# A five-buffer ring for the mixer outputs and x, and a split moved to GpSimd, in an S5/pooling diffusion step

## The chip, the core and the metric

The kernel runs on one core of one Trainium2 chip. The metric is device time in microseconds. A core has five engines that run their own instruction streams and meet through semaphores: TensorE (PE in the profile, with PEld for its weight loads), VectorE (DVE), ScalarE (ACT), GpSimd (POOL) and SyncE (SP), which here only issues DMAs. DMAs can be issued by SP, ACT and POOL. The matmul and vector instructions of one engine run in the order in which they stand in its stream, and that order is fixed when the kernel is built.

## The reference

Two token groups run through two layers: 128 context tokens and 1024 latent tokens, 1024 channels each, fp32.

```
for i in 0, 1:
    h = x * (1 + scale) + shift                       # adaLN, from silu(c) @ ada_w
    if i == 0:  s5 scan both ways, y = gelu(C s + D u)
                v = y @ glu_w + glu_b                 # 1024 -> 2048
                o = v[:, :1024] * sigmoid(v[:, 1024:])
    else:       multi-scale box means of h, minus h, times small weights
    x = layer_norm(4**0.25 * x + gate1 * o)
    f = (silu(m(x) @ w_gate) * (m(x) @ w_up)) @ w_down   # 1024 -> 2816 -> 1024
    x = layer_norm(4**0.25 * x + gate2 * f)
```

Outputs are both groups' x and the context's final scan states.

## The kernel before

The latent tokens are handled in two halves of 512, blocks A and B. The large products of A and B run on TensorE in a split form: each fp32 operand is written as a high part in fp32r (ScalarE, L828) plus a low part (VectorE, L829), and `mm` (L842 to L848) issues three matmuls, high x high (L844), high x low (L845), low x high (L846). The context block C (128 tokens) uses plain fp32 (L848); an fp32 matmul or transpose appears in the profile as two PE instructions.

The scan of layer 0 ends in `ssm_y`, called for the eight channel blocks in the order 6, 7, 5, 0, 1, 2, 3, 4. Each call forms y for all 1024 tokens, and eight DMAs on GpSimd's queue (L686) store it in the DRAM tensor yd[kt]. All of its tiles are in one memory pool (ssy), closed after the last call.

Then `build` opens the pools of the next stages in the memory that the scan leaves: split weights (wh, wl, three buffers), X (the residual stream), lat (work tiles of A and B, among them the ring hk of split hidden activations, three buffers of a high and a low part), xm (A's split operand) and glup. In glup lie xn (B's split operand) and the ring yr of two buffers of 128x1024 fp32. The loop at L1197 loads yd[k] for k = 0 to 7 in turn by GpSimd's queue (L1199) and splits it: tokens 0 to 511 into xm, tokens 512 to 1023 into xn, each with one ScalarE copy and one VectorE subtraction, 128x512, written with a stride of 8 elements since the scan's token order differs.

The gated unit (`glu`, L892) then takes A and B through eight output blocks m. A block m loads two weight tiles of 512 KB into the ring `raw` (three buffers, SP's queue, L837), splits them, and runs 2 x 8 x 3 = 48 matmuls of 512 columns over k = 0 to 7. Its result is gated (tile sg, two buffers) and added to X. For A, `load_x` (L410) is called at m = 0 for token tiles 0 to 3 and at m = 3 for tiles 4 to 7: each loads 128 rows of x into a buffer of the same ring `raw`, by SP's queue (L416), and TensorE transposes it (px, L421) into X.

Beside the gated unit runs `fill`: the context's feed-forward of layer 0, a generator stepped at points in the program (18 steps stand ahead of A's gated unit). In the gated unit it loads its weights, in pieces of 256 KB, into its own ring rc of three buffers (L1293). A tile framework orders the instructions when the kernel is built: by program order as priority, among those that its own timeline says are ready. It also adds the waits, among them that the tiles of a new pool wait for the pools whose memory they take.

After the gated unit come layer norm, up projection and down projection of A and of B (`ffn_down` splits the hidden activations into hk, L948), then layer 1.

Of the kernel before, what the change touches and what calls it, by code (L numbers as in the profile page):

```python
# [11 lines left out]
F32 = mybir.dt.float32  # L12
# [3 lines left out]
OP = mybir.AluOpType  # L16
# [25 lines left out]
class Kernel:  # L42
# [367 lines left out]
    def load_x(self, qs):  # L410

        nc = self.nc
        xs = self.I["x_sample"].rearrange("o n d -> (o n) d")
        for q in qs:
            xp = self.raw.tile([128, 1024], F32, tag="raw", name=f"xr{q}")
            nc.sync.dma_start(xp, xs[128 * q:128 * q + 128, :])  # L416
            for kh in range(2):
                px = self.psum("px")
                for k4 in range(4):
                    kt = 4 * kh + k4  # L420
                    nc.tensor.transpose(px[:, 128 * k4:128 * k4 + 128], xp[:, 128 * kt:128 * kt + 128], self.ident)  # L421
                nc.scalar.activation(self.X[q // 4][:, 4 * kh:4 * kh + 4, 128 * (q % 4):128 * (q % 4) + 128],
                                     px.rearrange("p (k n) -> p k n", k=4), AF.Copy)
# [497 lines left out]
    def ffn_down(self, b, l, h):  # L921
        nc, I = self.nc, self.I
        wd = I["ffn_w_down"][l].rearrange("(f p) d -> p f d", p=128)
        gate = self.gate[l, 1]

        def residual(ps, m):
            nc.vector.scalar_tensor_tensor(b.x[:, m, :], ps, gate[:, b.i, m:m + 1], b.x[:, m, :],
                                           op0=OP.mult, op1=OP.add)

        if not b.split:  # L930
            for m in range(8):
                ps = self.psum("dn", b.ps)[:, 0:b.n]
                for fo, fn in ((0, 8), (8, 8), (16, 6)):
                    w = self.weight(b, wd[:, fo:fo + fn, m * 128:m * 128 + 128], [128, fn, 128])
                    for f in range(fn):
                        self.mm(b, ps, [w[0][:, f, :]], [h[:, fo + f, :]], fo + f == 0, fo + f == NF - 1)
                residual(ps, m)
                yield m
            return
        for half in range(2):  # L940
            ps = [self.psum(f"dn{m}", b.ps)[:, 0:b.n] for m in range(4)]
            for f2 in range(NF // 2):
                w = self.weight(b, wd[:, 2 * f2:2 * f2 + 2, half * 512:half * 512 + 512], [128, 2, 512])
                nq = 512 // b.n
                for q in range(2):
                    f = 2 * f2 + q
                    if q % nq == 0:
                        hh = self.split(b.tmp, h[:, f:f + nq, :], [128, nq, b.n], "hk", 3)  # L948
                    for m in range(4):
                        self.mm(b, ps[m], [t[:, q, m * 128:m * 128 + 128] for t in w],  # L950
                                [t[:, q % nq, :] for t in hh], f == 0, f == NF - 1)
                yield f2
            for m in range(4):
                residual(ps[m], half * 4 + m)
# [204 lines left out]
    def build(self):  # L1159
        tc, nc = self.tc, self.nc  # L1160
        with ExitStack() as st:
# [25 lines left out]
            xr = P("xres")  # L1187
# [5 lines left out]
            with tc.tile_pool(name="xm1", bufs=1) as xmp:  # L1193
                xm = [xmp.tile([128, 8, 512], F32R, name=f"xm{q}") for q in range(2)]
                with tc.tile_pool(name="glup", bufs=1) as tmp:
                    xm2 = [tmp.tile([128, 8, 512], F32R, name=f"xn{q}") for q in range(2)]
                    for k in range(8):  # L1197
                        yr = tmp.tile([128, 1024], F32, tag="yr", name="yr", bufs=2)
                        nc.gpsimd.dma_start(yr, self.yd[k])  # L1199
                        yv = yr.rearrange("p (t c) -> p t c", t=8)  # L1200
                        tok = lambda a: a[:, k].rearrange("p (c t) -> p t c", t=8)
                        for q, x in enumerate((xm, xm2)):
                            self.split_into(tok(x[0]), tok(x[1]), yv[:, ::-1, 64 * q:64 * q + 64])
                    with tc.tile_pool(name="rawc", bufs=1) as self.rawc:
                        self.glu(A, xm, fill, hooks={0: range(4), 3: range(4, 8)})
                        self.glu(B, xm2, fill)
                        self.drain(fill)
                    self.rawc = None
                    self.ln(A, 0, 0, xm)
                    first = list(self.up_w(A, 0, 0))  # L1210
                self.cright.close()
                hpool = tc.tile_pool(name="ffna", bufs=1, side="right")
                h = hpool.__enter__().tile([128, NF, 512], F32, name="h")
                with tc.tile_pool(name="adl", bufs=1, side="right") as adl:
                    fill = self.ada_late(adl)
                    self.drain(self.ffn_up(A, 0, xm, h, first), fill)
                    self.ln_stats(B)
                    self.ln_apply(B, 0, 0, xm)
                    self.drain(self.ffn_down(A, 0, h), fill)
                    self.drain(fill)  # L1220
                self.drain(self.ffn_up(B, 0, xm, h))
                self.ln(A, 0, 1)
            mid, side = ExitStack(), ExitStack()
# [21 lines left out]
            xm = [xmp.tile([128, 8, 512], F32R, name=f"xp{q}") for q in range(2)]  # L1245
# [11 lines left out]
            h = st.enter_context(hp).tile([128, NF, 512], F32, name="h2")  # L1257
# [69 lines left out]
```

## Time and profile before

| | us |
|---|---|
| median of 3 runs (2425.71 to 2427.06) | 2426.21 |
| profiled execution | 2425.86 |
| its span | 2424.1 |
| PE busy | 2243.9 (93%) |
| VectorE busy | 1282.3 (53%) |
| ScalarE busy | 922.9 (38%) |
| GpSimd busy | 269.1 (11%) |

A busy share says what an engine spent its time on, not what bounded a stage. Here PE is the busy engine, and from about 541 us to the end it has little idle time; its gaps lie in the first quarter of the span, where the scan, its hand-over to the gated unit and the context's work are. Idle time of an engine other than the bound costs nothing by itself. The granted clock is TensorE's, as a share of 2.4 GHz.

### The profile page before, as it was taken

How to read it: one execution, taken by the hardware profiler on the slowest of the kernel's cores; microseconds unless marked ns; L12 is line 12 of the kernel's file. 1: busy time of each engine (PE TensorE's matmuls, PEld its weight loads, DVE VectorE, ACT ScalarE, POOL GpSimd, SP SyncE). 2: the span in 40 equal slices, each digit the busy share in tenths (PEclk: the TensorE clock that was granted, in tenths of full speed). 3: DMA queues.
4: the chain of work that ended last, by engine and by line, in shares of the span. 5: the costliest groups of instructions: out<-in, count | busy, mean ns of one | idle time of the engine just before them, and what ended most of it. 6: DMA issues, size and time to landing. Idle time of an engine off the chain costs nothing.

```text
span 2424.1 us, 33331 instructions
## 1 busy us (share of the span) xinstructions
PE 2243.9 (93%) x13105; PEld 1872.7 (77%) x13105; DVE 1282.3 (53%) x2420; ACT 922.9 (38%) x1376; POOL 269.1 (11%) x337
## 2 busy tenths in 40 slices
PE   4896679699999999999999998889999999999996
PEld 2565678688877777788888888777788888888996
DVE  6679964343555222557222765677422456322576
ACT  3674225442243222534222543226222443322464
POOL 4931336300010000100000010002000100000000
PEclk7996889899999999999999999999999999999998
DMA  7778459755544555432333226764333323333463
GB/s 223 238 238 229 140 166 262 223 177 165 150 137 149 164 183 165 167 99 87 103 98 96 96 96 174 220 196 133 105 96 96 96 97 95 96 98 102 140 200 104
DMA packets 457916, 357.22 MB, mean 147 GB/s; under 512 B 14864, under 2 KB 405792, under 8 KB 455712
## 3 DMA queue, kind: packets, MB, share of 16 engines
q1 hardware_dynamic: 451824, 340.90, 46.7%
q0 software_dynamic: 3200, 8.39, 1.1%
q10 hardware_dynamic: 2736, 5.80, 0.6%
q8 instruction: 103, 1.69, 0.3%
q14 instruction: 53, 0.43, 0.1%
HBM read 336.58 MB, written 18.35 MB: 146 GB/s over the span
## 4 chain that ended last, share of the span: by engine, by line
PE 81%; DMA 11%; DVE 3%; ACT 2%; issue 1%; POOL 1%; SPq 0%; ACTq 0%; POOLq 0%; DVEq 0%
PE ffn L844 13%; PE ffn L846 13%; PE ffn L845 13%; PE dn L845 6%; PE dn L844 6%; PE dn L846 6%; PE ffn L848 4%; PE dn L848 3%; PE glu L844 2%; PE glu L846 2%; PE glu L845 2%; DMA adaw<-ada_w 2%; DMA raw<-ffn_w_up 2%; DMA raw<-ffn_w_gate 1%; PE pvv L465 1%
## 5 line engine op out<-in xcount | busy, mean ns | idle before, releaser
L828 ACT ACTIVATE wh<-raw 128x1024 fp32r<-128x1024 f32 (+1 forms) x326 | 341.6, 1049 | 930.4 <-PE ffn L845 611.4
L829 DVE TENSOR_TENSOR wl<-raw,wh 128x1024 fp32r<-128x1024 f32 (+1 forms) x326 | 394.7, 1211 | 492.6 <-ACT wh L828 485.3
L845 PE MATMUL dn<-hkl,wh 128*128 128x512 f32 (+1 forms) x880 | 304.5, 348 | 0.3 <-DVE hkl L829 0.3
L846 PE MATMUL dn<-hkh,wl 128*128 128x512 f32 (+1 forms) x880 | 303.0, 347 | 0.0
L844 PE MATMUL ffn<-xp,wh 128*128 128x512 f32 x704 | 274.8, 391 | 2.2 <-ACT wh L828 2.2
L846 PE MATMUL ffn<-xp,wl 128*128 128x512 f32 x704 | 275.3, 391 | 0.5 <-DVE wl L829 0.5
L844 PE MATMUL ffn<-xm,wh 128*128 128x512 f32 x704 | 275.2, 392 | 0.0
L846 PE MATMUL ffn<-xm,wl 128*128 128x512 f32 x704 | 275.0, 391 | 0.0
L845 PE MATMUL ffn<-xp,wh 128*128 128x512 f32 x704 | 274.6, 391 | 0.0
L845 PE MATMUL ffn<-xm,wh 128*128 128x512 f32 x704 | 273.9, 389 | 0.0
L844 PE MATMUL dn<-hkh,wh 128*128 128x512 f32 (+1 forms) x880 | 262.5, 348 | 0.9 <-ACT hkh L828 0.9
L848 PE MATMUL ffn<-xmc,raw 128*128 128x128 f32 x1280 | 166.3, 287 | 33.7 <-DMA raw<-ffn_w_up 9.9
L918 DVE TENSOR_TENSOR h<-ffn,sg 128x512 f32<-128x512 f32 x88 | 60.7, 690 | 248.2 <-PE ffn L846 248.1
L848 PEld LDWEIGHTS ffn<-xmc,raw 128*128 128x128 f32 x1280 | 157.2, 200 | 43.9 <-DMA raw<-ffn_w_up 13.7
L845 PEld LDWEIGHTS dn<-hkl,wh 128*128 128x128 f32 x880 | 166.6, 189 | 21.1 <-DVE hkl L829 0.5
L846 PEld LDWEIGHTS dn<-hkh,wl 128*128 128x128 f32 x880 | 166.5, 189 | 20.4
L844 PEld LDWEIGHTS dn<-hkh,wh 128*128 128x128 f32 x880 | 163.3, 189 | 23.4 <-ACT hkh L828 1.7
L844 PEld LDWEIGHTS ffn<-xm,wh 128*128 128x128 f32 x704 | 132.1, 188 | 31.8 <-issue 4.3
L844 PEld LDWEIGHTS ffn<-xp,wh 128*128 128x128 f32 x704 | 132.5, 188 | 30.7 <-ACT wh L828 2.5
L846 PEld LDWEIGHTS ffn<-xp,wl 128*128 128x128 f32 x704 | 132.5, 188 | 28.9 <-DVE wl L829 1.0
L846 PEld LDWEIGHTS ffn<-xm,wl 128*128 128x128 f32 x704 | 132.1, 188 | 28.9 <-issue 0.7
L845 PEld LDWEIGHTS ffn<-xp,wh 128*128 128x128 f32 x704 | 132.4, 188 | 28.1 <-issue 0.5
(333 smaller groups left out, 3282.0 us busy)
## 6 DMA issues: line engine op xcount, KB each, us to landing
raw<-ffn_w_gate SPq DMA_DIRECT2D x128, 512.0 KB
raw<-ffn_w_up SPq DMA_DIRECT2D x128, 512.0 KB
raw<-ffn_w_down SPq DMA_DIRECT2D x126, 512.0 KB
adaw<-ada_w SPq DMA_DIRECT2D x96, 512.0 KB
raw<-ssm_glu_w SPq DMA_DIRECT2D x48, 512.0 KB
mo<-mo SPq DMA_DIRECT2D x14, 1024.0 KB
rc<-ffn_w_down SPq DMA_DIRECT2D x40, 256.0 KB
mo<-otab SPq DMA_DIRECT2D x32, 256.0 KB
```

The lines of the kernel that those rows point to most:

```text
L465: nc.tensor.matmul(pv[64 * x:64 * x + 64, 144 * r:144 * r + 144], tt[:, q, r, 64 * x:64 * x + 64], self.u[:, 2 * gp + x, :], start=True, s ...
L828: nc.scalar.activation(h, src, AF.Copy)
L829: nc.vector.tensor_tensor(l, src, h.bitcast(F32), op=OP.subtract)
L844: nc.tensor.matmul(ps, wh, xh, start=start, stop=False)
L845: nc.tensor.matmul(ps, wh, xl, start=False, stop=False)
L846: nc.tensor.matmul(ps, wl, xh, start=False, stop=stop)
L848: nc.tensor.matmul(ps, w[0], x[0], start=start, stop=stop)
L918: v.tensor_tensor(h[:, f, :], self.in_sb(b, v, pu), sg, op=OP.mult)
```

## The change

The ring yr has five buffers, stands first in its pool glup, and is reached through `self.yr`; two of its tiles are made before xn. `load_x` takes its tiles from this ring and issues its loads on GpSimd's queue. The second token half of each yd tile is split by GpSimd, with a copy and a subtraction; the first half stays on ScalarE and VectorE. The ring hk moves out of the pool lat into one of its own, on the other side of the memory, opened after the context's pools are closed and kept to the end; lat is 12 KB a partition smaller, so xm and the start of glup lie 12 KB lower, and glup, with three more buffers of 4 KB, ends where it ended.

```diff
     def load_x(self, qs):
         for q in qs:
-            xp = self.raw.tile([128, 1024], F32, tag="raw", name=f"xr{q}")
-            nc.sync.dma_start(xp, xs[128 * q:128 * q + 128, :])
+            xp = self.yr(f"xr{q}")
+            nc.gpsimd.dma_start(xp, xs[128 * q:128 * q + 128, :])
...
-                        hh = self.split(b.tmp, h[:, f:f + nq, :], [128, nq, b.n], "hk", 3)
+                        hh = self.split(self.hk, h[:, f:f + nq, :], [128, nq, b.n], "hk", 3)
...
                 with tc.tile_pool(name="glup", bufs=1) as tmp:
+                    self.yr = lambda n: tmp.tile([128, 1024], F32, tag="yr", name=n, bufs=5)
+                    yrs = [self.yr(f"yr{k}") for k in range(2)]
                     xm2 = [tmp.tile([128, 8, 512], F32R, name=f"xn{q}") for q in range(2)]
                     for k in range(8):
-                        yr = tmp.tile([128, 1024], F32, tag="yr", name="yr", bufs=2)
+                        yr = yrs[k] if k < 2 else self.yr(f"yr{k}")
                         nc.gpsimd.dma_start(yr, self.yd[k])
-                        yv = yr.rearrange("p (t c) -> p t c", t=8)
+                        yv = yr.rearrange("p (t c) -> p t c", t=8)[:, ::-1]
                         tok = lambda a: a[:, k].rearrange("p (c t) -> p t c", t=8)
-                        for q, x in enumerate((xm, xm2)):
-                            self.split_into(tok(x[0]), tok(x[1]), yv[:, ::-1, 64 * q:64 * q + 64])
+                        self.split_into(tok(xm[0]), tok(xm[1]), yv[:, :, 0:64])
+                        nc.gpsimd.tensor_copy(tok(xm2[0]), yv[:, :, 64:128])
+                        nc.gpsimd.tensor_tensor(tok(xm2[1]), yv[:, :, 64:128], tok(xm2[0]).bitcast(F32),
+                                                op=OP.subtract)
...
                 self.cright.close()
+                self.hk = st.enter_context(tc.tile_pool(name="hkp", bufs=1, side="right"))
```

## Rows read from the trace of the kernel before

**Rows 1.** Stretches of the span: each engine's busy us (instructions), granted clock, DMA share, GB/s.
```profile
core 0: us, PE busy (x) PEld busy (x) DVE busy (x) ACT busy (x) POOL busy (x), PEclk, DMA share, GB/s
...
448.80:461.68 12.88, 0.00 (x1) 0.03 (x1) 2.36 (x2) 2.02 (x3) 5.30 (x10) 0.70 0.55 167
461.68:472.00 10.32, 9.51 (x40) 8.71 (x41) 4.20 (x4) 5.21 (x6) 1.06 (x2) 0.54 0.75 235
472.00:504.00 32.00, 29.26 (x179) 24.98 (x178) 16.54 (x17) 21.60 (x26) 2.12 (x4) 1.00 0.76 238
504.00:531.00 27.00, 27.00 (x121) 22.33 (x121) 9.26 (x11) 8.61 (x10) 0.00 (x0) 1.00 0.41 124
531.00:541.20 10.20, 7.63 (x67) 7.14 (x65) 3.71 (x5) 6.49 (x11) 0.00 (x0) 1.00 0.77 228
```

**Rows 2.** PE's groups by form, 461.6 to 504: busy us, mean ns, idle before and releaser.
```profile
L848 PE MATMUL ffn<-xmc,rc 128*128 128x128 f32 x112 | 17.7, 308 | 13.7 <-DMA rc<-ffn_w_gate 12.9 <-DMA rc<-ffn_w_up 0.8
L845 PE MATMUL glu<-xm,wh 128*128 128x512 f32 x24 | 10.1, 422 | 0.4 <-DVE xm L829 0.3
L844 PE MATMUL glu<-xm,wh 128*128 128x512 f32 x25 | 9.7, 447 | 2.3 <-ACT xm L828 2.2
L846 PE MATMUL glu<-xm,wl 128*128 128x512 f32 x24 | 9.5, 394 | 0.0
L421 PE MATMUL px<-ident,xr 128*128 128x128 f32 x32 | 5.6, 317 | 0.0
```

**Rows 3.** Timeline of PE, 531 to 541: start us, us, instructions, idle before.
```profile
531.16 1.91 PE L421 MATMUL px<-ident,xr 128*128 128x128 f32 x16
...
537.67 1.06 PE L421 MATMUL px<-ident,xr 128*128 128x128 f32 x8 [1.05 <-ACT sg L916]
540.26 1.16 PE L848 MATMUL dn<-hc,rc 128*128 128x128 f32 x8 [1.52 <-DMA rc<-ffn_w_down]
541.17 0.48 PE L844 MATMUL glu<-xm,wh 128*128 128x512 f32 x1
```

**Rows 4.** The tile yr: durations in ns, minimum/median/maximum, and DMA us to landing.
```profile
L829 DVE TENSOR_TENSOR xm<-yr,xm x8: 1116/1174/1229, 466.6 to 498.9; 128x512 fp32r<-128x512 f32 x8
...
DMA to landing us min/median/max: 3.5/5.7/7.3
```

**Rows 5.** Timeline of ACT: the first and the last split of xm.
```profile
465.43 1.13 ACT L828 ACTIVATE xm<-yr 128x512 fp32r<-128x512 f32 x1 [14.61 <-DMA yr<-yd]
...
497.78 1.13 ACT L828 ACTIVATE xm<-yr 128x512 fp32r<-128x512 f32 x1 [4.28 <-DMA yr<-yd]
```

**Rows 6.** Timeline of POOL: stores of yd[0], of yd[4], and the first loads.
```profile
408.32 4.53 POOL L686 DMA_DIRECT2D yd<-yl  x8
...
451.12 4.18 POOL L686 DMA_DIRECT2D yd<-yl  x8 [3.12 <-ACT yl L683]
459.87 1.12 POOL L1199 DMA_DIRECT2D yr<-yd  x2 [4.57 <-issue]
```

**Rows 7.** Timeline of POOL, 34 to 49: two-input operations.
```profile
37.86 1.11 POOL L80 TENSOR_TENSOR oc<-pw,nct 128x512 f32<-128x512 f32 x1
...
43.37 1.96 POOL L76 TENSOR_TENSOR oc<-pw,ct 128x512 f32<-128x512 f32 x1
```

**Rows 8.** Timeline of DVE, 34 to 49: two-input operations.
```profile
38.90 1.23 DVE L77 TENSOR_TENSOR pb<-pq,bt 128x1024 f32<-128x1024 f32 x1 [1.05 <-ACT bt L318]
...
42.20 2.17 DVE L80 TENSOR_TENSOR pb<-pq,bt 128x1024 f32<-128x1024 f32 x1
```

**Rows 9.** Lines L1012 and L631: ns minimum/median/maximum, first and last start, forms.
```profile
L1012 POOL TENSOR_SCALAR lx<-X,lnm x32: 766/966/3784, 703.1 to 1911.5; 128x512 f32<-128x512 f32 x32
...
L631 POOL COPY sd<-Z x16: 1057/1562/1657, 349.1 to 441.8; 64x512 f32<-64x512 f32 x16
```

**Rows 10.** Timeline of SP's DMA queue: x tiles 4 to 7, the next glu weight.
```profile
507.82 24.73 SPq L416 DMA_DIRECT2D xr<-x_sample  x4
533.10 0.38 SPq L837 DMA_DIRECT2D raw<-ssm_glu_w  x1
```

**Rows 11.** Waits of SP's queue, 430 to 520: us in total, times, longest.
```profile
SPq L1293 <- DMA yd<-yl: 6.0, 4, 5.5
```

## The prediction, made before the change was run

> **What bounds the kernel now.** I read the table of stages first. TensorE (PE) is the bound: from 504 to 531 us it is busy all the time, 121 instructions in 27.00 us, all but one of them 512-column matmuls of the gated unit, so one costs 0.225 us at the full clock [rows 1]. The only place inside the change's reach where PE loses time is 448.8 to 541.2 us. Second view, PE's instructions by form from 461.6 to 504: 112 context-ffn and 32 transposes (fp32, 128x128) and 73 gated-unit matmuls [rows 2]. Eight fp32 ones take 540.26 to 541.17, so 0.113 each [rows 3]. Full-clock need: 144 x 0.113 + 73 x 0.225 = 16.3 + 16.4 = 32.7 us; elapsed from 461.68 to 504: 42.3. Lost: 9.6. In the first 10.32 us of it the granted clock was 0.54 [rows 1], about the 1.2 GHz level, after PE had stood for 12.88 us; at the full clock that work takes at most 10.32 x 0.54 = 5.6, so 4.7 of the 9.6 is the low clock and its gaps, and 4.9 falls between 472 and 504. From 531.2 to 541.2, PE has 64 fp32 instructions (67 less three glu): 7.2 us of work in 10.0, 2.8 lost, with two waits of 1.05 and 1.52 us, and not one glu matmul starts between 531.2 and 541.17 [rows 1, 3].
>
> So the ledger is 12.9 (PE empty) + 4.7 + 4.9 + 2.8 = 25.3 us, of a profiled execution of 2425.86 us (span 2424.1). The median of the runs is 2426.21, 0.35 above it.
>
> **The change part by part.**
>
> *Five buffers in place of two.* Eight mixer outputs yr0 to yr7 come through two buffers; each load waits until the splits of the one two before are done, then takes 3.5 to 7.3 us to land [rows 4]. So the first split starts at 465.43 and the last only at 497.78 [rows 5]: 32.4 us for eight. Five loads at once bring yr2 to yr4 forward. But the first stays where it is: yr0 reads yd[0], whose stores were issued at 408.32, and yet is issued at 459.87, right after the stores of yd[4] (issued 451.12 to 455.30) have landed [rows 6]. It waits for the memory of the stage before, not for its data; the new pool reaches into the same memory. I therefore leave the 12.9 us as they are, and with them the low clock behind them (4.7), which could shift by 1 or 2 us either way.
>
> yr0 to yr4 are issued from 459.87 on. Five times 512 KB at the 235 GB/s of that stretch [rows 1] would be 11 us, so yr4 lands by about 471. ScalarE's share falls from two splits a tile to one: 465.43 and then tile by tile to 472.
>
> *Second half split by GpSimd.* This removes eight 1.2 us instructions from ScalarE and eight from VectorE and puts sixteen on GpSimd. Neither engine is the bound, so the relief itself is worth nothing; what counts is when yr buffers come free. No row shows a GpSimd write with this 32-byte stride. From below: 1.10 us for a two-input 128x512 operation [rows 7] and 0.77 for a one-input one [rows 9], 1.9 us a tile. From above: 1.96 us each beside a busy VectorE [rows 7, 8] is 3.9, and one-input 3.78 at worst [rows 9] makes 5.9. VectorE pays for the same strided split 1.17 [rows 4], and a GpSimd copy with strided reads 1.56 [rows 9]. I take 1.5 + 1.9 = 3.4 us a tile, nearest to the strided copy.
>
> yr5 needs the first buffer, so the first tile's GpSimd split. In program order the splits of tiles 1 to 4 also stand ahead of load 5, and GpSimd works in order: if it keeps that order, yr5 to yr7 are issued at 465 + 5 x 3.4 = 482, land by 488 and are split by 490; if not, by 482. Today: 500. So the operand is whole 10 to 18 us sooner. Until then PE has tiles 0 to 4 for the first two output blocks (5 x 6 x 0.225 = 6.8 us for one, half of that again for the gate of the next) and some 80 of the fp32 context instructions (9 us) to fill about 20 us. I expect 1.5 to 3.5 us of the 4.9 to remain lost and take 2.3 as regained; from 0 to 4.9 is possible.
>
> VectorE and GpSimd also slow each other. At 38.90 a 128x1024 VectorE operation on two operands in memory took 1.23 us, at 42.20 the same form 2.17, with GpSimd at 1.96 beside it instead of 1.11 [rows 7, 8]. That is why I don't take 4.9: the low half of the A split on VectorE is in the same burst. The Trainium skill (SBUF — State Buffer, SBUF: two separate sides) says that a VectorE instruction with two SBUF inputs and a GpSimd instruction reading SBUF lock each other out for a whole instruction. The rows agree. Taken strictly, it makes a tile cost 1.17 + 3.4 = 4.6 us, load 5 goes out near 488, and nothing of the 4.9 comes back: the second rival.
>
> *x through the ring, on GpSimd's queue.* Today xr4 to xr7 take the three weight buffers in turn: SP's queue is held by them from 507.82 to 532.55, and the next glu weight is issued at 533.10 [rows 10]. That is the hole without a glu matmul [rows 3]. With weights alone in these buffers it closes: 2.8 us, between 0 (another fill order makes a like hole) and 2.8. I take 2.8. SP loses eight issues; GpSimd gains eight of the 0.56 us that its loads take [rows 6], 4.5 us behind its splits. What waits for them is the residual update of the first output block, and the two sg buffers let PE go on for two more blocks (11 us each), so x may come as late as 510 without cost. The transposes go: they no longer fill PE at 469 to 480, where the glu tiles now must. In bandwidth nothing is won: the bytes are the same. The Trainium skill (DMA: Bandwidth & Descriptors, Issuing engines are not separate DMA queues) says as much: transfers from all issuing engines share 16 DMA engines. The table shows these 0.75 busy [rows 1], so yr2 to yr4 push back the context weights; that is within my 1 or 2 us.
>
> *hk in its own pool.* The same instructions, tags and counts; nothing. Its memory is that of the context blocks, which finish beside the gated unit, a whole up projection before A's down projection needs hk. If that cover went, its first splits would wait a few us while PE is still in the up projection.
>
> Sum: 2.3 + 2.8 + 0 = 5.1. 2425.86 - 5.1 = 2420.8; against the median 2421.1. I give 2421.
>
> **Rivals.**
>
> *Memory sooner.* The ring now lies at the low end of its pool. Should its first two buffers not have to wait for the last stores, yr0 could go out at 455.3 behind them, or at 448.0 in GpSimd's gap: 4.6 to 11.9 us sooner, and PE starts on glu that much before 467. For: yd[0] is long written. Against: the context weights (rc), which have nothing to do with yd, also waited for its stores, once for 5.5 us [rows 11]. Time: 2409 to 2416.5.
>
> *Only the hole at 531.* GpSimd's splits and VectorE's take turns, yr5 to yr7 come as late as now, and the missing transposes leave PE with less to fill: 0 to 2.8 us are won. For: the slowed rows; against: three tiles more are there at 472. Time 2423 to 2426.
>
> *Slower.* GpSimd's splits cost over 5.3 us a tile. The last A split then ends at 465 + 5 x price + 8.5, which passes today's 500 from there on; at 7.6 (two of the longest, 3.78) it is 511.5, and the x loads behind it come past 515, when PE, in order, stands at their transposes and at the third output block. Loss 11.5, less 2.8, and about 2 that filler covers: 2432. For: 3.78 has happened [rows 9]. Against: the median there is 0.97.
>
> **How the numbers follow.** What a measurement of this kernel tells from no change is about 0.2%, 4.85 us: faster means below 2421.4. Forecast 0.50 (its own range 2418 to 2423.5: 0.31 faster, 0.19 same); memory sooner 0.13, faster; only the hole 0.20, same; slower 0.17 (0.16 slower, 0.01 same). Faster 0.44, same 0.40, slower 0.16. Leaving out 0.1 on either side: 2414 to 2429.5.
>
> **What would show it.** Right: yr0 to yr4 issued back to back after 459.5, the context weights still first on PE near 461.7, the last ScalarE split of A between 482 and 492, no x load on SP and no glu-free stretch of 10 us near 531. Wrong: yr0 issued before 456 (memory sooner); GpSimd splits above 5 us a tile, or PE waiting for transposes (slower); VectorE's A splits near 2.3 us with the last one after 497 (only the hole).

## The result, and the profile after

| | us |
|---|---|
| before, median beside it | 2425.96 |
| after, median of 4 runs (2438.0 to 2440.71) | 2439.32 |
| ratio after to before, 95% interval | 1.0053, 1.0040 to 1.0066 |
| measured again, 5 runs beside 11 of before | 1.0066, 1.0054 to 1.0078 |
| profiled execution after; its span | 2438.46; 2436.7 |

The change costs 13 to 16 us. The forecast was 5 us faster. Ratios here rest on undisturbed runs (an execution of 9204 us in *xr3_free* below is left out) and aren't quotients of the medians beside them, from which they can differ by a few us.

Where it goes is read from the same stretches as [rows 1]; the windows of the profile after, columns as there (its scan ends 2.2 us later, see below):

```profile
448.80:461.68 12.88, 2.22 (x20) 2.03 (x19) 3.50 (x3) 4.03 (x5) 5.65 (x11) 0.79 0.67 191
461.68:472.00 10.32, 3.75 (x16) 3.49 (x16) 0.46 (x1) 1.61 (x2) 4.33 (x7) 0.60 0.80 271
472.00:504.00 32.00, 27.10 (x156) 23.47 (x157) 11.34 (x10) 8.41 (x10) 26.71 (x20) 0.89 0.73 235
504.00:531.00 27.00, 19.32 (x114) 16.81 (x114) 5.75 (x7) 9.39 (x14) 4.18 (x6) 0.87 0.71 217
531.00:541.20 10.20, 10.20 (x46) 8.45 (x46) 3.87 (x4) 2.70 (x3) 0.00 (x0) 1.00 0.21 61
```

The hole of 531 to 541 is closed, as forecast (PE 10.20 of 10.20). A larger one stands at 504 to 531: PE 19.32 of 27.00, where it was busy throughout. The granted clock has changed too: 0.89 and 0.87 from 472 to 531, where it was 1.00 [rows 1]. What PE does there, the timeline of PE after (start us, us, instructions, idle before and its releaser):

```profile
505.36 0.73 PE L844 MATMUL glu<-xm,wh 128*128 128x512 f32 x2 [0.46 <-ACT xm L828]
...
507.57 1.04 PE L421 MATMUL px<-ident,xr 128*128 128x128 f32 x8
508.45 2.84 PE L848 MATMUL dn<-hc,rc 128*128 128x128 f32 x24
511.13 1.04 PE L421 MATMUL px<-ident,xr 128*128 128x128 f32 x8
513.51 1.16 PE L848 MATMUL dn<-hc,rc 128*128 128x128 f32 x8 [1.34 <-DMA rc<-ffn_w_down]
517.65 1.18 PE L848 MATMUL dn<-hc,rc 128*128 128x128 f32 x4 [2.98 <-DMA rc<-ffn_w_down]
521.27 2.07 PE L848 MATMUL dn<-hc,rc 128*128 128x128 f32 x8 [2.44 <-DMA rc<-ffn_w_down]
523.13 2.60 PE L421 MATMUL px<-ident,xr 128*128 128x128 f32 x16
525.49 0.47 PE L844 MATMUL glu<-xm,wh 128*128 128x512 f32 x1
```

The first output block m=0 ends at 507.5, the second begins at 525.49. Between them stand the transposes of x tiles 0 to 3 (px; a transpose is one PE instruction in these traces, a context matmul two) and matmuls of the context's down projection (dn). The waits there are for the context's weights (rc), not for x. PE's waits from 451 to 526 are almost all for these weights; of the first row 14.5 us are the empty stretch behind the scan, which was 12.9 before:

```profile
PE ffn L848 <- DMA rc<-ffn_w_gate: 18.7, 5, 14.5
PE dn L848 <- DMA rc<-ffn_w_down: 6.8, 3, 3.0
PE ffn L848 <- DMA rc<-ffn_w_up: 3.5, 3, 2.8
...
```

(us in all, times, longest).

The clock falls behind such waits. Windows of PE after (us, PE busy and its instructions, granted clock, DMA share, GB/s):

```profile
486.02:491.02 5.00, 2.32 (x17) 0.94 0.96 304
491.02:496.02 5.00, 5.00 (x28) 0.72 0.93 309
...
511.02:516.02 5.00, 2.30 (x19) 1.00 1.03 330
516.02:521.02 5.00, 1.18 (x4) 0.67 1.06 365
521.02:526.02 5.00, 4.75 (x26) 0.65 0.75 189
```

PE had been busy 2.32 of 5.00 us ahead of the first fall (0.72) and 2.30 and 1.18 ahead of and in the second (0.67, 0.65): part of these windows ran at the lower of the clock's two levels, 1.2 GHz in place of 2.4. In the kernel before, the clock stood at 1.00 from 472 to 541 [rows 1].

The tile yr after, to set beside [rows 4] (ns minimum/median/maximum, first and last start):

```profile
L1205 POOL CAST xn<-yr x8: 1100/1149/2219, 470.2 to 495.7; 128x512 fp32r<-128x512 f32 x8
...
L829 DVE TENSOR_TENSOR xm<-yr,xm x8: 1092/1406/2405, 471.5 to 505.3; 128x512 fp32r<-128x512 f32 x8
L1206 POOL TENSOR_TENSOR xn<-yr,xn x8: 1517/1579/4427, 472.4 to 509.5; 128x512 fp32r<-128x512 f32 x8
...
DMA to landing us min/median/max: 4.5/6.6/10.0
```

And GpSimd's queue after, the timeline of POOL that answers to [rows 6]:

```profile
463.93 2.68 POOL L1201 DMA_DIRECT2D yr<-yd  x5 [5.42 <-issue]
470.22 2.35 POOL L1205 CAST xn<-yr 128x512 fp32r<-128x512 f32 x2 [3.61 <-DMA yr<-yd]
...
482.22 0.57 POOL L1201 DMA_DIRECT2D yr<-yd  x1
...
490.73 0.57 POOL L1201 DMA_DIRECT2D yr<-yd  x1
491.30 0.54 POOL L416 DMA_DIRECT2D xr<-x_sample  x1
...
508.92 0.54 POOL L416 DMA_DIRECT2D xr<-x_sample  x1 [10.17 <-PE px L421]
509.47 1.55 POOL L1206 TENSOR_TENSOR xn<-yr,xn 128x512 fp32r<-128x512 f32 x1
```

Load 5 goes out at 482.22, the forecast 482; but load 7 only at 490.73, and x tile 3 at 508.92, since it got the buffer of x tile 0 and waits for its transposes; GpSimd's last split stands behind that wait. ScalarE's last split of A is at 504.19, before at 497.78 [rows 5]; ACT's timeline after:

```profile
504.02 0.28 ACT L916 ACTIVATE sg<-ffn 128x128 f32<-128x128 f32 x1 [7.23 <-PE ffn L848]
504.19 1.11 ACT L828 ACTIVATE xm<-yr 128x512 fp32r<-128x512 f32 x1
```

Its tile had been there since 495.74 at the latest, when GpSimd copies from it. The split stood behind an activation of the context on ScalarE, and that waited for PE's context matmuls.

One thing about comparing such traces. The end of the scan, the last matmul py, falls anywhere from 441.8 to 456.3 us in the 16 profiles read here, in a stretch whose code the edits leave alone. So I compare from there on. Lines of the tiles py and glu (last number: last start), of the kernel before:

```profile
L680 PE MATMUL py<-sd,mo x256: 274/275/421, 354.0 to 448.5; 128*128 128x128 f32 x128
L844 PE MATMUL glu<-xm,wh x128: 387/389/774, 468.0 to 597.4; 128*128 128x512 f32 x128
```

and of the changed one:

```profile
L680 PE MATMUL py<-sd,mo x256: 274/275/421, 353.2 to 450.7; 128*128 128x128 f32 x128
L844 PE MATMUL glu<-xm,wh x128: 389/389/774, 473.0 to 613.7; 128*128 128x512 f32 x128
```

From the end of the scan to the end of A's gated unit: 148.9 us before, 163.0 after. The profiled spans differ by 12.6 us: the scan ends 2.2 us later after, this stretch is 14.1 longer, and what follows it is 3.7 shorter (it takes 1823.0 to 1830.2 us in the 16 profiles). So the stretch holds the loss. The table below gives it for every kernel.

### The profile page after: what moved, and what is told of

It is laid out like the page before. It is cut to its first block, busy times and chain, and to the rows that moved or that the text cites. A ratio compares the mean times of both kernels' runs of the same rounds, so it can differ in the third digit from the quotient of the medians.

```text
span 2436.7 us, 33334 instructions
## 1 busy us (share of the span) xinstructions
PE 2240.1 (92%) x13105; PEld 1870.1 (77%) x13105; DVE 1279.5 (53%) x2412; ACT 910.0 (37%) x1364; POOL 299.3 (12%) x361
## 4 chain that ended last, share of the span: by engine, by line
PE 81%; DMA 12%; DVE 3%; ACT 2%; POOL 1%; issue 1%; SPq 0%; ACTq 0%; DVEq 0%; POOLq 0%
PE ffn L844 13%; PE ffn L846 13%; PE ffn L845 13%; PE dn L844 6%; PE dn L845 6%; PE dn L846 6%; PE ffn L848 4%; PE dn L848 3%; PE glu L845 2%; PE glu L846 2%; PE glu L844 2%; DMA adaw<-ada_w 2%; DMA raw<-ffn_w_gate 2%; DMA raw<-ffn_w_down 1%; DMA raw<-ffn_w_up 1%; PE pvv L465 1%
## 5 line engine op out<-in xcount | busy, mean ns | idle before, releaser
L846 PEld LDWEIGHTS ffn<-xp,wl 128*128 128x128 f32 x704 | 132.5, 188 | 28.7 <-DVE wl L829 1.0
```

Of the source, the lines that this page charges most:

```text
L846: nc.tensor.matmul(ps, wl, xh, start=False, stop=stop)
```

## The experiments

First theory: x tiles come late behind the mixer loads and GpSimd's splits, and block m=1 stands behind their transposes. Main rival: GpSimd's splits hold back the mixer tiles, and x has no part. The ratio is to the kernel before, run beside it (95% interval); "stretch" is from the last py to the last A glu as above, against 148.9, each from one profile; "ahead" counts the context matmuls that stand on TensorE behind the scan and ahead of block m=1, and ahead of its end (the 49th and the 96th of A's gated matmuls; the traces agree). *hk_only*, which has the order of the kernel before, differs from it by 2.7 in the stretch, so differences of up to 3 us there tell nothing; nor do ratios that lie within some 0.002 of each other.

| kernel | ratio | stretch | ahead |
|---|---|---|---|
| before | 1 | 148.9 | 32, 56 |
| hk_only | 1.0001 (0.9985 to 1.0017) | -2.7 | 32, 56 |
| ring5_only | 0.9999 (0.9987 to 1.0011) | -1.0 | 24, 28 |
| no_pool_split | 0.9984 (0.9969 to 0.9998) | -2.5 | 36, 36 |
| no_split_px_bank | 0.9982 (0.9965 to 0.9998) | -2.4 | 18, 28 |
| no_x_move | 1.0011 (0.9997 to 1.0026) | +2.6 | 27, 60 |
| x_ring_sp | 1.0015 (0.9998 to 1.0032) | +2.0 | 72, 72 |
| pool_copy_only | 1.0024 (1.0010 to 1.0038) | +2.8 | 60, 60 |
| px_bank | 1.0031 (1.0016 to 1.0046) | +5.7 | 28, 64 |
| xr3_dn_gate | 1.0043 (1.0027 to 1.0059) | +9.7 | 64, 64 |
| dn_gate | 1.0046 (1.0029 to 1.0063) | +10.8 | 64, 64 |
| after, again | 1.0066 (1.0054 to 1.0078) | +13.4 | 90, 90 |
| fixed_slots | 1.0068 (1.0055 to 1.0081) | +16.6 | 102, 102 |
| xr3_free | 1.0071 (1.0058 to 1.0084) | +18.1 | 94, 94 |
| no_dve_split | 1.0073 (1.0058 to 1.0089) | +11.7 | 86, 86 |

**The parts one by one.** *no_x_move*: x back to the weight buffers.

```diff
-            xp = self.yr(f"xr{q}")
-            nc.gpsimd.dma_start(xp, xs[128 * q:128 * q + 128, :])
+            xp = self.raw.tile([128, 1024], F32, tag="raw", name=f"xr{q}")
+            nc.sync.dma_start(xp, xs[128 * q:128 * q + 128, :])
```

> The changed kernel, but x goes back to the weight buffers on SP's queue; ring of five, GpSimd split and hk pool stay. Theory (x tiles come late: they stand on GpSimd's queue behind the last mixer tiles and GpSimd's splits, and the second gated-unit block stands behind their transposes on TensorE): the 525 us start of block m=1 goes back to below 510, the transposes run again at 469 to 485, and most of the 13.4 us loss goes: 2422 to 2430. Rival (GpSimd's splits hold the mixer tiles back, x has no part): the loss stays, 2434 to 2441, with x early and gated-unit matmuls of k=5 to 7 still late.

*no_pool_split*: the second half split by ScalarE and VectorE.

```diff
-                        nc.gpsimd.tensor_copy(tok(xm2[0]), yv[:, :, 64:128])
-                        nc.gpsimd.tensor_tensor(tok(xm2[1]), yv[:, :, 64:128], tok(xm2[0]).bitcast(F32),
-                                                op=OP.subtract)
+                        self.split_into(tok(xm2[0]), tok(xm2[1]), yv[:, :, 64:128])
```

> The changed kernel, but the second half is split by ScalarE and VectorE as before; ring of five, x through it on GpSimd's queue and hk pool stay. Theory (x late because its loads queue behind the mixer loads): without the splits GpSimd only issues, so loads 5 to 7 and x go out as soon as a ring buffer is free; x tile 3 still needs a buffer that x or the last mixer tiles free, so block m=1 starts about 512 to 520 and a part of the loss stays: 2430 to 2436. Rival (GpSimd's splits alone are the loss): 2420 to 2427.

*ring5_only* takes both edits, so that the ring of five buffers and the hk pool are left; *hk_only* is the kernel before with `self.hk` opened as in the change.

> Only the ring of five buffers and the hk pool; split on ScalarE and VectorE, x in the weight buffers on SP's queue. Theory: neither of the two loss-makers is there; the operand is whole by 485 to 492 and up to 4.9 us of the loss before 504 comes back: 2420 to 2425. Rival (five loads at once delay the context's weights and the start, whatever splits them): 2427 to 2432.

> The kernel before with only the hk ring in a pool of its own. Theory: nothing before 540 us changes and hk costs nothing: 2424 to 2428, within 0.1% of before. Rival (the new pool or the shifted memory makes a wait or another order after the gated unit): outside 2421 to 2431.

Measured: 2431.46, 2421.70, 2426.14 and 2426.78 us beside 2425.84. The hk pool costs nothing that these runs can tell, and the ring alone changes nothing (2426.14, above the 2420 to 2425 that I expected). To the ring, GpSimd's split adds 0.0012 of 2426, 2.9 us (5.3 by the medians); x through the ring takes 0.0015 off, 3.6 us (4.4 by the medians). Neither is clear of the noise by itself. Added up that is within 1 us of before; measured together they are 13 to 16 us over it. So neither part is the loss: it is what they make together, and neither theory had that. (*no_x_move*, 2431.46, lies above my theory's 2430 and below the rival's 2434; *no_pool_split* is where the rival had it and far below my 2430.) Without GpSimd's split the time is the one that I forecast for the whole change (2421.7; the forecast was 2421), though not by its sum, as the table of lost time below shows. GpSimd's queue in *no_pool_split*:

```profile
454.86 2.69 POOL L1201 DMA_DIRECT2D yr<-yd  x5 [5.25 <-issue]
465.20 0.53 POOL L1201 DMA_DIRECT2D yr<-yd  x1 [7.66 <-DVE xn L829]
...
469.47 0.53 POOL L1201 DMA_DIRECT2D yr<-yd  x1 [1.66 <-DVE xn L829]
471.59 0.53 POOL L416 DMA_DIRECT2D xr<-x_sample  x1 [1.59 <-DVE xn L829]
```

A buffer comes free every 2.1 us, all eight mixer loads are out 14.6 us after the first, against 26.8 in the changed kernel (463.93 to 490.73), and x follows at once. PE is then busy 30.27 of 32.00 us and all of the next 27.00, at the full clock (this profile's scan ends 6.7 us sooner than that of before, so the same windows lie that much later in the stage):

```profile
472.00:504.00 32.00, 30.27 (x166) 25.13 (x166) 16.26 (x18) 20.82 (x26) 3.81 (x8) 1.00 0.78 242
504.00:531.00 27.00, 27.00 (x163) 23.84 (x162) 9.15 (x10) 13.75 (x18) 0.00 (x0) 1.00 0.47 137
```

**Between the two.** *px_bank*: the changed kernel with `px = self.psum("px", "s")`, so the transposes of x use a PSUM bank of their own. *x_ring_sp*: its x loads by `nc.sync`. *pool_copy_only*: GpSimd's subtraction by `nc.vector`. *no_split_px_bank*: no_pool_split with the px edit.

> The changed kernel whole, GpSimd split too; only the transposes of x go to the idle one-buffer PSUM bank s in place of the five-buffer ring of the gated unit, so block m=1 no longer stands behind x in PSUM, and the built order puts most of m=1 ahead of the transposes. Theory (x comes late behind GpSimd's splits, and TensorE loses the time because m=1 stands behind x): m=1 runs before 510 whether x is there or not, the context fill is not used up early, and 8 to 12 of the 13.4 us come back: 2426 to 2431. Rival (the loss is the operand: mixer tiles 5 to 7 come late behind the splits, m=1 needs them as much as m=0): under 3 us come back, 2436 to 2440.

> The changed kernel whole, but the x loads into the ring are issued by SP's queue, so they don't stand behind GpSimd's instructions; they still wait for the ring's buffers. Theory, first form (the queue's order is what delays x): x tiles 0 to 3 go out by 490 to 500 and half or more of the loss comes back, 2426 to 2433. Second form (the buffers are what delays x: each is free only when GpSimd has done its slow subtraction on it): x goes out as late as in the changed kernel, and the time stays at 2435 to 2441.

> The changed kernel, but GpSimd makes only the high part of the second half (1.1 us a tile), VectorE makes the low part. Theory (the price of GpSimd's split of a tile sets when ring buffers come free and when load 5 goes out): a tile costs GpSimd under half, load 5 goes out by about 476, the last split of the first half ends by 490, x is there by 500, and most of the loss is gone: 2421 to 2428. Rival (any GpSimd work between the loads is enough, by the queue's order): 2432 or more.

> The changed kernel with the second half split by ScalarE and VectorE (2421.7 measured) and the transposes of x in the idle PSUM bank. Theory: x is there by 487 and TensorE waits for it only 0.7 us, so nothing is left for the bank to win: 2420 to 2424, within 0.1% of that kernel. Rival (a gated-unit block ahead of the transposes fills the remaining gaps): 2414 to 2419.

Measured: 2432.43, 2429.02, 2431.59 and 2420.01 beside 2425.30. The last was as expected, and *x_ring_sp* fits its first form. *px_bank* gave back 5 to 8 us, a little less than expected. *pool_copy_only* halves GpSimd's work, gets load 5 out at 473.57 and the last A split 38.2 us after the scan's end (487.1, 448.9) for 53.5 in the changed kernel, and is still 6 us over: a miss, and a sign that the operand alone is not it. What it still waits for stands between its transposes of x, at weights of the context:

```profile
502.54 2.08 PE L848 MATMUL ffn<-xmc,rc 128*128 128x128 f32 x8 [2.87 <-DMA rc<-ffn_w_up]
```

In *x_ring_sp* the first four x loads are issued 43.0 to 52.2 us after the scan's end (486.6 to 495.8, scan's end 443.6), so the last of them 6 us sooner than in the changed kernel (40.6 to 58.2), and most of the loss is gone. Whether x or the order did that, this run can't tell: the order on PE has changed with it. 24 of the 32 transposes stand ahead of the end of m=0, where they fill PE while the context's weights come, and of the down projection only eight matmuls stand ahead of m=1.

**x or the order.** *fixed_slots* and *xr3_free* make the ring's buffers go strictly in turn; *xr3_free* also takes x tiles 4 to 7 off GpSimd's queue. *no_dve_split* takes VectorE's part of the first half away: a second ScalarE copy stands in its place, so the low part of that half is left out. The edit of *xr3_free*, without the lines that hand each yr tile its number:

```diff
-            xp = self.yr(f"xr{q}")
-            nc.gpsimd.dma_start(xp, xs[128 * q:128 * q + 128, :])
+            xp = self.yr(f"xr{q}", 8 + q)
+            (nc.gpsimd if q < 4 else nc.sync).dma_start(xp, xs[128 * q:128 * q + 128, :])
...
-                    self.yr = lambda n: tmp.tile([128, 1024], F32, tag="yr", name=n, bufs=5)
+                    self.yr = lambda n, i: tmp.tile([128, 1024], F32, tag=f"yr{i % 5}", name=n, bufs=1)
...
```

> The changed kernel once more, beside the three others of this call, since its first time rests on four runs. Both theories: 2434 to 2441, 8 to 15 us over the kernel before.

> The changed kernel with the five buffers as five tiles taken strictly in turn, so x tile 3 takes the buffer of mixer tile 6 and not that of x tile 0. In GpSimd's built order the load of x tile 5, which waits for the transposes of x tile 0, then stands ahead of the last split and of x tile 3. Theory (GpSimd works in order: any load that waits for TensorE's transposes holds up x tile 3 and with it block m=1): nothing is won, 2434 to 2441. Rival (only the buffer of x tile 3 was wrong): 2426 to 2432.

> As the kernel with buffers in turn, but x tiles 4 to 7 are issued by SP's queue: on GpSimd's queue no load that waits for TensorE stands ahead of x tiles 0 to 3; the splits stay ahead of them. Theory: x tile 3 goes out at about 500 in place of 509, block m=1 starts near 512 in place of 525, and 7 to 11 us of the loss come back: 2426 to 2432. Rival (x tiles are late by the splits alone, whatever stands behind): 2434 to 2441.

> The changed kernel with the low part of the first half written by a ScalarE copy instead of VectorE's subtraction (the low part of that half is left out), so VectorE reads nothing of the ring while GpSimd splits. Theory (VectorE and GpSimd hold each other up): GpSimd's copies take 1.1 and its subtractions 1.5 us throughout, none over 2, the load of mixer tile 5 goes out by 478, some 4 us sooner, and the time falls by 2 to 6 us to 2430 to 2436; the wait for x tile 3 stays. Rival (GpSimd's long instructions have another cause, as the strided write): instructions of 2.2 to 4.4 us stay and load 5 goes out at 482, 2435 to 2441.

Measured: 2441.52, 2442.61, 2443.96 and 2443.86 beside 2426.59. The changed kernel lies 0.5 us above its range. In *fixed_slots* nothing is won, as expected, though it lies 1.6 us above its range. *xr3_free* refutes my first theory, which had 2426 to 2432 for it. x tile 3 goes out 50.2 us after the scan's end (497.90), 8 us sooner than in the changed kernel; the x tiles of this run land in at most 6.2 us, so it is there by 505, and nothing is won. PE in *xr3_free*:

```profile
512.01 1.04 PE L421 MATMUL px<-ident,xr 128*128 128x128 f32 x8
514.18 1.16 PE L848 MATMUL dn<-hc,rc 128*128 128x128 f32 x8 [1.14 <-DMA rc<-ffn_w_down]
516.84 0.71 PE L848 MATMUL dn<-hc,rc 128*128 128x128 f32 x4 [1.50 <-DMA rc<-ffn_w_down]
517.74 1.96 PE L848 MATMUL dn<-hc,rc 128*128 128x128 f32 x8 [0.19 <-DMA rc<-ffn_w_down]
519.50 1.91 PE L421 MATMUL px<-ident,xr 128*128 128x128 f32 x8
524.01 1.45 PE L848 MATMUL dn<-hc,rc 128*128 128x128 f32 x8 [2.59 <-DMA rc<-ffn_w_down]
525.25 1.91 PE L421 MATMUL px<-ident,xr 128*128 128x128 f32 x8
```

No transpose waits for x here. PE, in order, comes to them through down-projection matmuls whose weights arrive one piece of 256 KB (eight of these instructions) in some 3 us. *no_dve_split* bears on the contention of VectorE and GpSimd, for which I had expected 2430 to 2436: a miss. With VectorE off the ring GpSimd's instructions stay short:

```profile
L1206 POOL CAST xn<-yr x8: 1101/1116/1238, 468.1 to 488.1; 128x512 fp32r<-128x512 f32 x8
...
L1207 POOL TENSOR_TENSOR xn<-yr,xn x8: 1512/1557/1609, 471.0 to 505.6; 128x512 fp32r<-128x512 f32 x8
```

Load 5 goes out 26.4 us after the scan's end (476.06, 449.7) where the changed kernel has 31.5, the last A split comes 7 us sooner, and the time is no better than the changed kernel's (its one profile has the stretch 2 us shorter). The contention shows in the rows, and taking it away wins nothing.

**The order itself.** New theory: TensorE's order was built (by the tile framework, the planner below) with the context's matmuls where the plan had a wait for late x, and PE stands at their weights. The next edit makes the first down-projection weights (layer 0, first output block of the context) wait for the first residual update of A: VectorE first writes one element of X, `after`, into each of their buffers. *dn_gate* puts it into the changed kernel, *xr3_dn_gate* into *xr3_free*. Its core:

```diff
         for q, t in enumerate(tiles):
             c = min(4, n - 4 * q)
+            if after is not None:
+                nc.vector.tensor_copy(t[:, 0, 0:1], after)
             nc.sync.dma_start(t[:, 0:c, :], src[:, 4 * q:4 * q + c, :])
```

> The changed kernel, but the first weights of the context's down projection may load only after the first residual update of block A (a one-element VectorE write into each of their buffers reads X first), so in TensorE's order 64 context matmuls stand ahead of block m=1 in place of 90, and none that waits for down-projection weights stands between the transposes. x stays as late as in the changed kernel: tile 3 goes out near 508 and lands near 518. Order theory alone (TensorE stands at context weights written ahead of m=1): m=1 starts by 512 and most of the loss goes, 2426 to 2432. Two-cause theory (x late, and the order planned for a late x): m=1 waits for x until about 520 and under 5 us come back, 2434 to 2440.

> Both at once: x tile 3 goes out at about 498 (buffers in turn, x tiles 4 to 7 on SP's queue) and the context's down projection can't stand ahead of m=1. Two-cause theory: m=1 starts by 510 in place of 527, TensorE's idle time between 505 and 525 (7 to 10 us) goes, and of the 17 us that the kernel with the early x tile alone has over before 8 to 13 go: 2430 to 2436. Rival (neither is the cause; the late operand is): 2438 to 2444.

Measured: 2436.83 and 2437.39 beside 2425.67. With x late, the order gives back 0.0020, 4.9 us, against the changed kernel measured again, but only 0.0007 against its first measurement, so no gain is shown there; m=1 starts at 514.86, between the marks of the two theories (512 and 520). With x early it gives back 0.0028, 6.8 us (expected 8 to 13, so I had it too large; the time lies between the two ranges). This is clear of the noise by little, and the stretch agrees (18.1 to 9.7). x early gives nothing under either order (0.0046 and 0.0043 over before; 0.0066 and 0.0071), so of the two causes that I expected there x falls. The transposes in *xr3_dn_gate* now run one after the other, and m=1 starts 64.6 us after the scan's end (515.08, 450.5) for 74.8 in the changed kernel:

```profile
508.44 1.03 PE L421 MATMUL px<-ident,xr 128*128 128x128 f32 x8
...
510.25 1.48 PE L421 MATMUL px<-ident,xr 128*128 128x128 f32 x12
513.16 2.09 PE L421 MATMUL px<-ident,xr 128*128 128x128 f32 x12 [1.44 <-ACT sg L899]
515.08 0.50 PE L844 MATMUL glu<-xm,wh 128*128 128x512 f32 x1
```

Where the rest sits shows in PE's lost time: elapsed time less 0.113 us for each fp32 instruction and 0.226 for each 512-column matmul that starts in it. In every kernel the stretch holds the same 324 and 381 of these, so the lost times add up to the differences in the stretch (to some 0.2 us). Columns by us after the scan's end; "clock" is the time from 30 us on times what the granted clock lacks of 1.00, the most that the lower clock can have cost.

| lost, us | to 35 | 35 to 60 | 60 to 80 | 80 to the end | in all | clock |
|---|---|---|---|---|---|---|
| before | 19.6 | 3.1 | 0 | 3.3 | 25.9 | 0 |
| no_pool_split | 20.7 | 2.6 | 0 | 0.1 | 23.4 | 0 |
| no_x_move | 20.9 | 3.1 | 0 | 4.6 | 28.5 | 1.7 |
| x_ring_sp | 21.6 | 6.0 | 0.1 | 0.1 | 27.8 | 0 |
| pool_copy_only | 21.4 | 7.1 | 0.1 | 0.1 | 28.7 | 1.7 |
| px_bank | 22.1 | 8.2 | 0 | 1.4 | 31.6 | 1.7 |
| changed | 21.5 | 8.7 | 9.5 | 0.2 | 39.9 | 5.1 |
| xr3_free | 21.6 | 12.6 | 9.4 | 0.4 | 44.0 | 8.5 |
| dn_gate | 21.6 | 11.0 | 4.0 | 0.2 | 36.7 | 5.1 |
| xr3_dn_gate | 21.6 | 11.6 | 2.3 | 0.2 | 35.6 | 1.7 |

The changed kernel loses 1.9 us more at the start, 5.6 more between 35 and 60, where block m=0 waits for its last operand tiles (k = 5 to 7), and 9.5 more between 60 and 80, ahead of m=1; it gains 3.1 behind, where the hole was. The loss ahead of m=1 is the down projection in PE's order, with the clock that falls behind its waits: *xr3_dn_gate* takes it from 9.4 to 2.3, and the clock's share, at most 8.5 in *xr3_free*, to at most 1.7. How much of the gain is shorter waiting and how much the clock can't be told apart. *px_bank* has nothing lost there either. The loss between 35 and 60 stays in both. In the changed kernel PE has only the context's matmuls to run there until the last operand tiles come, and it waits for their weights. What that loss needs is not settled. *no_x_move*, with its last A split 47.7 us after the scan's end (504.0, 456.3; before 49.3; changed 53.5), loses no more than before; its transposes and part of m=1 stand there. But *pool_copy_only*, with the operand whole at 38.2, loses 7.1, so a late operand is not a condition.

Still open: why the planner places them so. That its own timeline has x late after GpSimd's splits fits the counts (90 ahead with the splits, 36 without), but was argued, not tried. And the count is not all: *x_ring_sp* has 72 ahead and loses little, and *xr3_dn_gate* and *dn_gate* with 64 lose more than it. Open too is why the weights come so slowly ahead of m=1. From 511 to 521 the DMA engines were full (share 1.03 and 1.06, at 330 and 365 GB/s), and four x tiles (508.92 to 513) and two weight tiles of the gated unit (509.95 and 512.37), 512 KB each, had been issued beside them. That this crowd of loads, rather than the order on PE, sets the wait is a rival that no run here separates.

## Why the prediction was wrong

- **Right**: yr0 to yr4 go out back to back (463.93; 2.68 us). GpSimd's split of the first five tiles ran from 470.22 to 488.86 with two issues of 0.57 between: 17.5 us, 3.5 a tile for the 3.4 taken. The hole at 531 closed: the last part of the stretch loses 0.2 us where it lost 3.3, for the 2.8 taken, and with x back in the weight buffers it is there again (4.6, *no_x_move*). hk cost nothing that can be told from noise (1.0001). The start did not move forward; PE stood for 14.5 us in place of 12.9.
- **The step that failed**: "What waits for them is the residual update of the first output block, and the two sg buffers let PE go on for two more blocks, so x may come as late as 510 without cost." The transposes are instructions of PE and stand in its order ahead of block m=1; the gated unit's PSUM buffers are theirs too, and with the transposes in another bank m=1 moves ahead of them and 5 to 8 us come back (px_bank). So "PE has tiles 0 to 4 for the first two output blocks" failed with it: no matmul of m=1 ran before 525.49. I counted what waits for x's data and not where the transposes stand on PE.
- **"The transposes go: they no longer fill PE at 469 to 480, where the glu tiles now must."** I named it and priced it at nothing. The order filled that place with context matmuls. PE ran 180 context instructions ahead of m=1 after, 111 before up to 503.8, from where the gated unit runs alone; the 69 more are 8.6 pieces of 256 KB, 2.3 MB. At the 217 to 235 GB/s of these stretches that is, as an estimate, some 10 us of transfer that the old order had spread over the next blocks. What PE lost in that place is measured: 9.5 us between 60 and 80 us after the scan's end, where it had lost nothing, with at most 5.1 us of the whole loss from the clock that fell behind the waits. The prediction had no term for the clock there.
- **Operand whole at 490, worth 2.3**: it was 504.19, and the stretch from 35 to 60 lost 8.7 us where it had lost 3.1. Load 7 stood behind five more of GpSimd's instructions, to 490.73; its tile came in time for 496, and then ScalarE's split of it stood 8 us behind the context's activation. Bringing the last split forward by 7 us won nothing (no_dve_split); by 15 us, with GpSimd's part halved, 7 to 10 of the 13 to 16 (pool_copy_only).
- **Luck**: load 5 went out at 482.22 for the forecast 482, but GpSimd's first split began at 470.22 and not at 465, and the load stood behind four copies and two subtractions and not behind five whole splits; the two errors cancel. *no_pool_split* ran at the time that was forecast, but not by the forecast's sum. The hole gave back 3.2 us for 2.8; the operand, whole 35.2 us after the scan's end in place of 49.3, gave 0.5 for 2.3.
- **The rival "slower"** named the place (PE in order at x's transposes) and about half the size (2432; 11.5 less 4.8, so 6.7 us for 13 to 16). But I made it hang on GpSimd's price, over 5.3 us a tile, and that is not its condition: it came at 3.5.
- **"Only the hole"** rested on VectorE and GpSimd holding each other up. The slowed rows came true (2.4 and 4.4 us at the longest), and with VectorE's subtractions off these tiles GpSimd's were short again (1.61 at the longest, *no_dve_split*). The Trainium skill (SBUF — State Buffer, SBUF: two separate sides) says that a VectorE instruction with two SBUF inputs and a GpSimd instruction that reads SBUF lock each other out. The trace agrees: the long ones, 4.43 and 2.41 us, stand only where both engines split. They weren't the cause of the loss: without them the time stayed (1.0073).

## What to carry to other kernels

An instruction that is moved takes its place in the order of every engine that handles its data: when a load is moved to a later place, find the instructions that use it on the bound engine and read what stands behind them there. A filler has its own price, its bytes: when work that needs no new weights leaves a gap, see what the planner puts there and how fast that can be fed. Waits on the bound engine can cost a second time, when the granted clock falls behind them (here at most 5.1 us). And two edits that are each harmless have to be measured together: here -3.6 and +2.9 us, neither clear of noise, made +13 to +16. The change without GpSimd's split (0.9984, 0.9969 to 0.9998) is faster than the kernel before by some 4 us, just clear of noise; with the transposes' bank moved as well it is the same (0.9982, 0.9965 to 0.9998).

## What the hardware did that I had not expected

GpSimd's strided split is quick when VectorE does not work on the same tiles: a 128x512 copy 1.10 to 1.24 us and a subtraction 1.51 to 1.61 (no_dve_split), where VectorE's same subtraction takes 1.17. Beside VectorE's subtractions the same instructions took up to 2.22 and 4.43 us, and VectorE's up to 2.41. With five 512 KB loads issued at once the mixer tiles landed in up to 10.0 us, where two at a time took at most 7.3 [rows 4]. The granted clock, 1.00 from 472 to 541 in the kernel before, fell to 0.72 and 0.65 in windows that followed windows with PE busy 2.32 and 1.18 of 5.00 us. And the scan's end, 14 us apart between two profiles, is a larger spread than most effects here: in single profiles only stretches counted from a common mark could be compared.
